# Whole 2048-column weight blocks in one cast and one subtraction, an opening over sixteen tiles, and decay rows by way of DRAM

## The chip, the cores and the metric

The kernel runs on one core of one Trainium2 chip. The metric is the device time of one execution in microseconds (us), the median of three runs. The engines are named as in the profile: PE is TensorE (PEld its weight loads), DVE is VectorE, ACT is ScalarE, SP is SyncE, which issues all DMAs here.

## What is computed

A trunk of two layers on 256 tokens of width 1024, in float32. Each layer has three sub-layers: a SwiGLU feed-forward of width 2816, a token mixer, and a second feed-forward. Each sub-layer is normalised, shifted and scaled by vectors that depend on a conditioning vector c, and added back through a gate. Cut to what matters here:

```python
def modulate(h, shift, scale):
    return h * (1 + scale[:, None, :]) + shift[:, None, :]

def swiglu(h, w13, w2):
    a, b = jnp.split(h @ w13, 2, axis=-1)
    return (jax.nn.silu(a) * b) @ w2

# layer 0: FFN half, mixer A/B (pooling + chunked state space), FFN half
# layer 1: FFN half, latent attention, FFN half
# c -> silu(c) @ mod_w[layer] + mod_b[layer]: nine vectors of 1024 per layer

# in the state-space mixer, per head and chunk of 128 tokens:
a_cs = jnp.cumsum(adt, axis=-1)
decay = jnp.exp(jnp.where(causal, a_cs[..., :, None] - a_cs[..., None, :], -jnp.inf))
```

## The kernel before

**Layout.** Activations lie transposed: channel on the partition, 256 tokens along the free axis, so a 1024-wide vector is 8 chunks. All weights are read once, in blocks of 128 x 2048 float32 (1 MB, sixteen 128 x 128 tiles), in the order of one list, `items` (lines 94 to 129). An item "w" is a weight block, "m" a block of `mod_w` (two halves of 1024 columns, one per chunk of one modulation vector), "f" a block that is used as it is. SP loads items in order into `RAHEAD` = 6 buffers `raw` (`issue_dma`, line 168).

**Splitting.** A float32 weight is used as a high part and a rest. `process_half` (line 188) takes half a "w" block: ACT casts 1024 columns into `wh` (line 217), DVE subtracts to get `wl` (line 218); each half has its own pair of buffers, 5 of each. For an "m" half, DVE multiplies it by silu(c) and sums along the row (line 204). `take` (line 239) hands out the next tile to PE and first sees that 4 pieces (halves) from the current one on have been written out in the program (`LOOK`). The order of instructions on an engine is then set by a planner with a cost model, by readiness and program order; line 207 pins each "m" product behind the vector instruction ahead of it in the program.

**Matmuls.** Most projections take three passes of 256 columns per tile (`mm3`, lines 254 to 256); the down projections two, of 512 and 256 (`mm2`, lines 260 and 261).

**The opening.** `first_pairs` (line 443) starts the first feed-forward before its modulation is complete. For each of four blocks of two chunks it waits for the four "m" halves of that block, scales and shifts two chunks (lines 397, 457), splits them (lines 308, 309) and multiplies eight output tiles by full-precision float32 products straight from an "f" block (line 465). The squares for the norm are summed by eight float32 products with a matrix of ones (line 315, called from `rms_r`). `ffn` (line 473) then goes through the 22 pairs of output tiles; the first four pairs are there already, the rest take `lin` twice. The vector c is loaded as a copy to all 128 partitions (line 148).

**The decay rows.** In `mixer_ab` (line 547), the cumulative sums of 16 heads are transposed to 16 rows (line 641), split into `ath` and `atl` (lines 643, 644), and for each head two PE products with a selecting column (lines 711, 712) spread the head's row over 128 partitions in PSUM. `heads` (line 705) makes the decay matrices from it on ACT (lines 718 to 722) and DVE (line 723), `ymm` (line 727) uses them. `heads`, tiles of z, and `ymm` take turns in the loop of line 772.

The lines of the list that set the start:

```python
    for b in range(4):
        items.append(mod_block(0, 1, b))
        items.append(mod_block(0, 0, b))
        items.append(("f" if b < NATIVE else "w", w13s[b], 4 * NS))
```

Of the kernel before, what the change touches and what calls it, by code (L numbers as in the profile page):

```python
# [17 lines left out]
P = 128  # L18
# [12 lines left out]
NS = 4  # L31
NATIVE = 4
# [6 lines left out]
MODS = (11, 10, 3, 0, 8, 8, 8, 8, 3, 1, 4)  # L39
# [22 lines left out]
def trunk(ctx, tc, xT, c_row, pos, kc, cols, rows, mod_w, w13s, w13, w2, win_a, wdt,  # L62
# [8 lines left out]
    sp = ctx.enter_context(tc.tile_pool(name="sp", bufs=4))  # L71
    pp = ctx.enter_context(tc.tile_pool(name="pp", bufs=8, space=bass.MemoryType.PSUM))
# [18 lines left out]
    def mod_block(l, v, b):  # L91
        return ("m", l, v, b)
# [68 lines left out]
    RAHEAD = 6  # L161
    PT = 8
    raws = {}
    state = {"dma": 0, "item": 0, "half": 0, "pin": False}
# [3 lines left out]
    def issue_dma(upto):  # L168
        while state["dma"] < min(upto, len(items)):
# [3 lines left out]
            if it[0] in "wf":  # L173
                nc.sync.dma_start(r[:, : it[2] * P], it[1])
            else:
                nc.sync.dma_start(r, mod_w[it[1], it[2], it[3]])
            raws[i] = r
            state["dma"] = i + 1
            if i == 15:
                late_loads()  # L180
# [7 lines left out]
    def process_half():  # L188
# [10 lines left out]
        if it[0] == "m":  # L199
            _, l, v, b = it  # L200
            c0 = l * 72 + v * 8 + b * 2 + hf
# [7 lines left out]
            if last:  # L209
                done_mod[(l, v, b)] = True  # L210
# [26 lines left out]
    LOOK = 4  # L237

    def take(m=1):
        if cur["off"] == 0:  # L240
            while len(pieces) < cur["piece"] + LOOK and process_half():
                pass
        wh, wl, n = pieces[cur["piece"]]
        o = cur["off"]
        cur["off"] += m
        assert cur["off"] <= n
        if cur["off"] == n:
            cur["piece"] += 1
            cur["off"] = 0
# [19 lines left out]
    def mod_col(l, v, part=ALL):  # L269
        lo, hi = part  # L270
        assert done_mod.get((l, v, hi // 2 - 1)), (l, v)
# [79 lines left out]
    class Norm:  # L351
# [30 lines left out]
        def sum_squares(self):  # L382
            sq = [tmp(f"sq{self.key}_{c}") for c in range(NC)]
            for c in range(NC):
                A.activation(sq[c], xt[:, c], AF.Square)  # L385
            self.r = rms_r(self.key, sq, 1.0 / D)
# [54 lines left out]
    NU = 3  # L441

    def first_pairs(norm):
        pts = [ps(f"n{m}") for m in range(2 * NS)]
        h32 = [slab(9 + q, f"h32_{q}", F32, [4, S]) for q in range(2)]
        for b in range(4):
            while not done_mod.get((0, 0, b)):
                process_half()
            if b == 0:
                norm.sum_squares()  # L450
            norm.gs = prep_scale(0, 0, (2 * b, 2 * b + 2))
            norm.sh = prep_shift(0, 0, (2 * b, 2 * b + 2))
            hs = []
            for c in (2 * b, 2 * b + 1):
                t = norm.scaled(c)
                h = h32[c // 4][:, c % 4]
                A.activation(h, t, AF.Identity, bias=norm.sh[:, c : c + 1])
                split(hh[:, c], hl[:, c], h)
                hs.append(h)
# [789 lines left out]
```

## Time and profile before

| what | us |
|---|---|
| median of 3 runs (1047.49 to 1048.79) | 1048.3 |
| the profiled execution | 1047.39 |
| its span | 1045.6 |
| PE busy | 1021.7 (98% of the span) |
| DVE busy | 837.1 (80%) |
| ACT busy | 569.0 (54%) |
| DMA | 253.46 MB, mean 242 GB/s |

The span is the time from the first to the last instruction of the profiled execution; the time of the execution is 1.8 us more. A busy PE means that some matmul is under way, and matmuls overlap, so the time that one of them takes on PE is read from the distance of starts in the timeline, not from its length.

### The profile page before, as it was taken

How to read it: one execution, taken by the hardware profiler on the slowest of the kernel's cores; microseconds unless marked ns; L12 is line 12 of the kernel's file. 1: busy time of each engine (PE TensorE's matmuls, PEld its weight loads, DVE VectorE, ACT ScalarE, POOL GpSimd, SP SyncE). 2: the span in 40 equal slices, each digit the busy share in tenths (PEclk: the TensorE clock that was granted, in tenths of full speed). 3: DMA queues.
4: the chain of work that ended last, by engine and by line, in shares of the span. 5: the costliest groups of instructions: out<-in, count | busy, mean ns of one | idle time of the engine just before them, and what ended most of it. 6: DMA issues, size and time to landing. Idle time of an engine off the chain costs nothing.

```text
span 1045.6 us, 18361 instructions
## 1 busy us (share of the span) xinstructions
PE 1021.7 (98%) x7386; PEld 955.3 (91%) x7386; DVE 837.1 (80%) x1508; ACT 569.0 (54%) x978; POOL 0.2 (0%) x4
## 2 busy tenths in 40 slices
PE   5999999999999999999999999999999999999997
PEld 4899998899888999998899999988988799999986
DVE  5788889989989897778879777899888689666553
ACT  3444454458786554445446444454678665444542
POOL 0000000000000000000000000000000000000000
PEclk9999999999999999999999999999999999999999
DMA  9999889965543577768875777798643246656501
GB/s 376 404 351 326 319 293 348 342 229 191 204 160 121 170 266 290 280 248 325 286 267 197 290 271 287 253 340 323 242 155 129 81 162 242 235 211 238 173 32 41
DMA packets 36102, 253.46 MB, mean 242 GB/s; under 512 B 4144, under 2 KB 4656, under 8 KB 5680
## 3 DMA queue, kind: packets, MB, share of 16 engines
q1 hardware_dynamic: 36016, 252.28, 65.8%
q8 instruction: 58, 0.95, 0.3%
q14 instruction: 28, 0.23, 0.1%
HBM read 251.22 MB, written 1.05 MB: 241 GB/s over the span
## 4 chain that ended last, share of the span: by engine, by line
PE 91%; DVE 5%; ACT 2%; DMA 1%; issue 0%; SPq 0%; DVEq 0%; ACTq 0%
PE f L260 16%; PE f L261 8%; PE a L254 7%; PE b L255 7%; PE b L254 7%; PE b L256 7%; PE a L256 7%; PE a L255 7%; PE o L260 3%; DVE raw L204 2%; PE o L261 2%; PE s L990 1%; DVE wl L218 1%; PE u_a L255 1%; PE u_a L254 1%; PE u_b L255 1%
## 5 line engine op out<-in xcount | busy, mean ns | idle before, releaser
L218 DVE TENSOR_TENSOR wl<-raw,wh 128x1024 fp32r<-128x1024 f32 x321 | 389.3, 1218 | 120.9 <-ACT wh L217 114.2
L217 ACT CAST wh<-raw 128x1024 fp32r<-128x1024 f32 x321 | 333.0, 1047 | 219.2 <-issue 89.0
L260 PE MATMUL f<-g,wh 128*128 128x512 f32 x704 | 248.9, 399 | 0.0
L261 PE MATMUL f<-g,wl 128*128 128x256 f32 x704 | 197.7, 281 | 0.0
L204 DVE SCALAR_TENSOR_TENSOR raw<-raw,c_bc 128x1024 f32<-128x1024 f32 x144 | 172.8, 1216 | 8.9 <-ACT sq L385 8.9
L254 PE MATMUL a<-hx,wl 128*128 128x256 f32 x600 | 170.0, 284 | 0.0
L255 PE MATMUL b<-hx,wh 128*128 128x256 f32 x600 | 169.8, 283 | 0.0
L256 PE MATMUL b<-hx,wh 128*128 128x256 f32 x600 | 169.8, 283 | 0.0
L254 PE MATMUL b<-hx,wl 128*128 128x256 f32 x600 | 169.8, 283 | 0.0
L256 PE MATMUL a<-hx,wh 128*128 128x256 f32 x600 | 169.7, 283 | 0.0
L255 PE MATMUL a<-hx,wh 128*128 128x256 f32 x600 | 169.5, 283 | 0.0
L260 PEld LDWEIGHTS f<-g,wh 128*128 128x128 f32 x704 | 132.3, 188 | 32.9
L261 PEld LDWEIGHTS f<-g,wl 128*128 128x128 f32 x704 | 133.0, 189 | 0.0
L254 PEld LDWEIGHTS a<-hx,wl 128*128 128x128 f32 x600 | 115.1, 192 | 0.6 <-ACT hx L391 0.6
L256 PEld LDWEIGHTS b<-hx,wh 128*128 128x128 f32 x600 | 115.2, 192 | 0.0
L255 PEld LDWEIGHTS b<-hx,wh 128*128 128x128 f32 x600 | 115.2, 192 | 0.0
L254 PEld LDWEIGHTS b<-hx,wl 128*128 128x128 f32 x600 | 115.2, 192 | 0.0
L256 PEld LDWEIGHTS a<-hx,wh 128*128 128x128 f32 x600 | 115.1, 192 | 0.0
L255 PEld LDWEIGHTS a<-hx,wh 128*128 128x128 f32 x600 | 115.1, 192 | 0.0
L504 ACT ACTIVATE s<-a 128x256 f32<-128x256 f32 x75 | 28.7, 383 | 94.6 <-PE a L256 94.6
L308 ACT CAST g<-g 128x256 fp32r<-128x256 f32 x88 | 35.4, 404 | 35.8 <-DVE g L505 27.1
L260 PE MATMUL o<-hx,wh 128*128 128x512 f32 x128 | 45.4, 398 | 0.0
(382 smaller groups left out, 1601.1 us busy)
## 6 DMA issues: line engine op xcount, KB each, us to landing
raw<-in_w SPq DMA_DIRECT2D x128, 1024.0 KB, 5.1
raw<-in_mod_w SPq DMA_DIRECT2D x72, 1024.0 KB, 5.3
raw<-in_win_a SPq DMA_DIRECT2D x12, 1024.0 KB, 6.6
raw<-in_wout_a SPq DMA_DIRECT2D x6, 1024.0 KB, 7.1
raw<-in_wq SPq DMA_DIRECT2D x5, 1024.0 KB, 4.9
raw<-in_w13s SPq DMA_DIRECT2D x4, 1024.0 KB, 10.3
raw<-in_win_m SPq DMA_DIRECT2D x4, 1024.0 KB, 7.1
raw<-in_wo SPq DMA_DIRECT2D x4, 1024.0 KB, 4.8
```

Source lines behind the costliest of these rows:

```text
L204: V.scalar_tensor_tensor(out=sl, in0=sl, scalar=1.0, in1=c_bc, op0=ALU.mult, op1=ALU.mult, accum_out=modc[:, c0 : c0 + 1])
L217: A.copy(wh[:, :n], src)
L218: V.tensor_tensor(out=wl[:, :n], in0=src, in1=wh[:, :n].bitcast(F32), op=ALU.subtract)
L254: T.matmul(pt, wl, xh, start=first, stop=False)
L255: T.matmul(pt, wh, xl, start=False, stop=False)
L256: T.matmul(pt, wh, xh, start=False, stop=last)
L260: T.matmul(pt, wh, x, start=first, stop=False)
L261: T.matmul(pt[:, S:], wl, x[:, 0], start=False, stop=last)
L308: A.copy(dh, src)
L504: A.activation(s, pa[:, :S], AF.Silu)
L990: T.matmul(pts[e][:, lo : lo + n], q[:, lo : lo + P], kk[:, 0:n], start=True, stop=False)
```

## The change

- A "w" block is cast by one instruction of 2048 columns and subtracted by one, into buffers of 8 KB, three of each; `LOOK` becomes 2 blocks. Inside the opening the work is still issued by halves (`fine`), into the same block buffers. `RAHEAD` becomes 5.
- `first_pairs` is rewritten: sixteen output tiles (eight pairs), issued in an order written out by hand and kept (`manual_schedule`). The first two chunks come one by one, each with its own halves of scale and shift; for eight tiles they are multiplied in full precision, for the other eight from a split block. The blocks of chunks 2 to 7 take three passes for all sixteen tiles. c is loaded as one row and spread by two PE products with ones; three and fourteen products with ones are added ahead of and behind the sum of squares; part of the squares goes to DVE.
- The decay rows: `acT` is written to DRAM and read back to all partitions, 8 heads per DMA, into `uh` and `ul`, which are free at that time; the selecting products go.
- `MODS` starts with (10, 11) in place of (11, 10): one "m" block moves from the first up projection to the first down projection.

The diff, cut to its core:

```diff
-NS = 4
-NATIVE = 4
+NS = 8
+NSETS = 2
...
+MODS = (10, 11, 3, 0, 8, 8, 8, 8, 3, 1, 4)
 NQ = 3
...
     cp = ctx.enter_context(tc.tile_pool(name="cp", bufs=1))
-    wp = ctx.enter_context(tc.tile_pool(name="wp", bufs=5))
...
+    def mod_block(l, v, b, halves=(0, 1)):
+        return ("m", tuple((l, v, b, h) for h in halves))
 
     items = []
-    for b in range(4):
-        items.append(mod_block(0, 1, b))
-        items.append(mod_block(0, 0, b))
-        items.append(("f" if b < NATIVE else "w", w13s[b], 4 * NS))
+    for c in range(2):
+        items += [("m", ((0, 1, 0, c), (0, 0, 0, c))), ("f", w13s[0, 0][:, 8 * P * c : 8 * P * c + 8 * P], 8)]
+    items.append(("w", w13s[1, 0], 16))
+    for b in range(1, 4):
+        items += [mod_block(0, 1, b), mod_block(0, 0, b)]
+        items += [("w", w13s[q, b], 16) for q in range(NSETS)]
...
     V.memset(wdtr, 0.0)
 
-    nc.sync.dma_start(c_bc, c_row.partition_broadcast(P))
+    crow = slab(10, "crow", F32, [D])[0:1]
+    nc.sync.dma_start(crow, c_row)
+    for q in range(2):
+        nc.sync.dma_start(xt[:, 4 * q : 4 * q + 4], xT[:, 4 * q : 4 * q + 4])
     nc.sync.dma_start(colt, cols)
-    A.activation(c_bc, c_bc, AF.Silu)
-    nc.sync.dma_start(xt, xT)
...
         nc.sync.dma_start(wkrr, wkr)
 
...
-            lo, hi = hf * PT, min((hf + 1) * PT, it[2])
-            n = (hi - lo) * P
-            wh = wp.tile([P, PT * P], F32R, tag="wh", name=f"wh{i}_{hf}")
-            wl = wp.tile([P, PT * P], F32R, tag="wl", name=f"wl{i}_{hf}")
-            src = r[:, lo * P : hi * P]
-            A.copy(wh[:, :n], src)
-            V.tensor_tensor(out=wl[:, :n], in0=src, in1=wh[:, :n].bitcast(F32), op=ALU.subtract)
-            pieces.append((wh, wl, hi - lo))
-            last = hi == it[2]
+            n = it[2]
+            lo, hi = (hf * PT, hf * PT + PT) if state["fine"] else (0, n)
+            if lo == 0:
+                cur["pair"] = [wp.tile([P, 2 * PT * P], F32R, tag=t, name=f"{t}{i}") for t in ("wh", "wl")]
+            wh, wl = cur["pair"]
+            o = slice(lo * P, hi * P)
+            A.copy(wh[:, o], r[:, o])
+            V.tensor_tensor(out=wl[:, o], in0=r[:, o], in1=wh[:, o].bitcast(F32), op=ALU.subtract)
+            pieces.append((wh, wl, lo, hi))
+            last = hi == n
...
-    LOOK = 4
+    LOOK = 2
+    state["look"] = LOOK
...
+    W0, W1 = 3, 14
 
     def first_pairs(norm):
-        pts = [ps(f"n{m}") for m in range(2 * NS)]
-        h32 = [slab(9 + q, f"h32_{q}", F32, [4, S]) for q in range(2)]
-        for b in range(4):
-            while not done_mod.get((0, 0, b)):
+        state["look"] = 1
+        wm = ps("warm")
+
+        def warm(n):
+            for _ in range(n):
+                T.matmul(wm[:, :P], onesf, onesf, start=True, stop=True)
+
+        def silu_c(q):
+            pt = ps(f"c{q}")
...
+            o = slice(512 * q, 512 * q + 512)
+            T.matmul(pt, onesf[0:1, :], crow[:, o], start=True, stop=True)
+            A.activation(c_bc[:, o], pt, AF.Silu)
+
+        warm(W0)
+        sq = [tmp(f"sq{c}") for c in range(NC)]
+        silu_c(0)
+        for c in (0, 1):
+            A.activation(sq[c], xt[:, c], AF.Square)
+        silu_c(1)
+        for c in (4, 5):
+            A.activation(sq[c], xt[:, c], AF.Square)
+        warm_sqrt("first")
...
+        for i, c in enumerate((0, 1, 2, 4, 5, 6)):
+            T.matmul(pss[:, :S], onesf, sq[c], start=i == 0, stop=i == 5)
+        warm(W1)
+        process_half()
+        r = sp.tile([P, S], F32, tag="r", name="r_first", bufs=2)
+        q = sp.tile([P, S], F32, tag="rq", name="rq_first", bufs=1)
+        v = sp.tile([P, 8], F32, tag="rv", name="rv_first", bufs=2)
+        V.transpose(q, pss[:, :S])
+        A.activation(v, q.rearrange("p (b j) -> p b j", j=32)[:, :, 0], AF.Sqrt, bias=eps_t[:, 0:1], scale=1.0 / D)
+        process_half()
+        V.reciprocal(v, v)
+        V.transpose(r.rearrange("p (b j) -> p b j", j=32), v.unsqueeze(2).to_broadcast([P, 8, 32]))
...
+        def scaled(c):
+            m, b = mod_col(0, 1, (c, c + 1))
+            g = gs_t[:, 0, c : c + 1]
+            V.scalar_tensor_tensor(out=g, in0=m, scalar=b1[:, c : c + 1], in1=colt[:, CP_NG + c : CP_NG + c + 1],
+                                   op0=ALU.add, op1=ALU.mult)
+            t = tmp(f"h{norm.key}_{c}")
+            V.tensor_tensor(out=t, in0=xt[:, c], in1=r, op=ALU.mult)
+            sh = prep_shift(0, 0, (c, c + 1))[:, c : c + 1]
+            A.activation(h[c], t, AF.Identity, bias=sh, scale=g)
+            A.copy(hh[:, c], h[c])
...
+        def low(c):
+            V.tensor_tensor(out=hl[:, c], in0=h[c], in1=hh[:, c].bitcast(F32), op=ALU.subtract)
...
+        def part(q, b):
+            for m in range(8 * q, 8 * q + 8):
+                for k in (2 * b, 2 * b + 1):
+                    wh, wl = take()
+                    for w, x in ((wl, hh), (wh, hl), (wh, hh)):
+                        T.matmul(tile_of(m), w, x[:, k], start=k == 0 and m % 2 == 0 and w is wl,
+                                 stop=k == NC - 1 and w is wh and x is hh, skip_group_check=True)
...
+        for c in range(2):
+            if c:
                 process_half()
+                process_half()
+            scaled(c)
+            w = next_raw()
+            for m in range(8):
+                T.matmul(tile_of(m), w[:, m * P : (m + 1) * P], h[c], start=c == 0 and m % 2 == 0, stop=False,
+                         skip_group_check=True)
+            release_raw()
+        low(0)
+        low(1)
+        process_half()
+        process_half()
+        part(1, 0)
+        for b in range(1, 4):
+            process_half()
+            process_half()
+            process_half()
+            scaled(2 * b)
+            process_half()
+            low(2 * b)
+            scaled(2 * b + 1)
+            process_half()
+            low(2 * b + 1)
+            for q in range(NSETS):
+                part(q, b)
+        while len(pieces) < cur["piece"] + 2:
+            process_half()
+        state["look"], state["fine"] = LOOK, False
+        norm.gs, norm.sh = gs_t[:, 0], sh_t[:, 0]
+        return [tile_of(m) for m in range(2 * NS)]
...
-        ath, atl = wd[0:16, 1], wd[0:16, 2]
-        V.tensor_copy(ath, pT[0:16, :S])
-        V.tensor_tensor(out=atl, in0=pT[0:16, :S], in1=ath.bitcast(F32), op=ALU.subtract)
+        acT = sp.tile([16, S], F32, tag="acT", name="acT", bufs=1)
+        V.tensor_copy(acT, pT[0:16, :S])
+        acd = dp.tile([1, 16, S], F32, name="acd")
+        nc.sync.dma_start(acd[0], acT)
+        rows_ = [t[:, :, :S].bitcast(F32) for t in (uh, ul)]
+        for q in range(2):
+            nc.sync.dma_start(rows_[q], acd[0:1, 8 * q : 8 * q + 8].partition_broadcast(P))
...
-                row = ps(f"row{h}")
-                sel = identr[0:16, h : h + 1].to_broadcast([16, P])
-                T.matmul(row[:, :S], sel, atl, start=True, stop=False)
-                T.matmul(row[:, :S], sel, ath, start=False, stop=True)
+                row = rows_[h // 8][:, h % 8]
...
-    pts = first_pairs(n)
+    with tc.manual_schedule(engines={mybir.EngineType.PE, mybir.EngineType.DVE, mybir.EngineType.Activation}):
+        pts = first_pairs(n)
```

## Rows read from the trace of the kernel before

**Rows 1.** The page of the profile: busy time and chain.

```profile
PE 1021.7 (98%) x7386; PEld 955.3 (91%) x7386; DVE 837.1 (80%) x1508; ACT 569.0 (54%) x978; POOL 0.2 (0%) x4
...
PE 91%; DVE 5%; ACT 2%; DMA 1%; issue 0%; SPq 0%; DVEq 0%; ACTq 0%
```

**Rows 2.** Waits of PE: who was waited for, us in total, times, longest.

```profile
PE ss L315 <- ACT sq L385: 8.3, 1, 8.3
PE n L465 <- ACT h L457: 5.8, 3, 4.5
...
PE o L1018 <- ACT pT L1012: 0.6, 2, 0.3
```

**Rows 3.** Timeline of the opening: start, length, engine, line, operation, count.

```profile
7.82 2.56 ACT L385 ACTIVATE sq<-xt 128x256 f32<-128x256 f32 x8 [1.87 <-DMA xt<-in_xT]
...
8.29 5.41 PE L315 MATMUL ss<-sq,onesf 128*128 128x256 f32 x16 [8.29 <-ACT sq L385]
...
18.16 15.77 PE L465 MATMUL n<-h,raw 128*128 128x256 f32 x64 [4.46 <-ACT h L457]
```

**Rows 4.** Timeline of PE: a native stretch, and starts of looped pairs.

```profile
42.49 7.17 PE L465 MATMUL n<-h,raw 128*128 128x256 f32 x32 [0.94 <-ACT h L457]
...
55.25 0.28 PE L254 MATMUL a<-hx,wl 128*128 128x256 f32 x1
...
72.53 0.28 PE L254 MATMUL a<-hx,wl 128*128 128x256 f32 x1
```

**Rows 5.** Windows: stretch, busy (count) of each engine, granted clock, DMA share, GB/s.

```profile
2.00:7.80 5.80, 0.00 (x0) 0.00 (x0) 0.00 (x0) 1.06 (x2) 0.00 (x0) 1.00 1.01 347
8.00:18.00 10.00, 5.41 (x16) 4.19 (x16) 6.89 (x16) 4.37 (x11) 0.00 (x0) 1.00 1.01 427
19.00:22.00 3.00, 3.00 (x9) 2.37 (x8) 2.96 (x7) 0.11 (x1) 0.00 (x0) 0.50 1.03 426
22.00:26.00 4.00, 4.00 (x21) 3.51 (x19) 3.57 (x9) 0.29 (x1) 0.00 (x0) 1.00 1.02 422
```

**Rows 6.** Timeline of DVE: subtractions of 256 and of 1024 columns.

```profile
35.05 0.76 DVE L309 TENSOR_TENSOR hx<-h,hx 128x256 fp32r<-128x256 f32 x2 [1.27 <-ACT hx L308]
...
48.88 2.35 DVE L218 TENSOR_TENSOR wl<-raw,wh 128x1024 fp32r<-128x1024 f32 x2
```

**Rows 7.** Timeline of PE in the first mixer: rows of two heads.

```profile
286.85 0.38 PE L711 MATMUL row<-wd,identr 16*128 16x256 f32 x1
...
287.52 0.38 PE L254 MATMUL z<-hx,wl 128*128 128x256 f32 x1
```

**Rows 8.** Windows: first down projection and mixers, columns as in Rows 5.

```profile
153.00:216.00 63.00, 63.00 (x361) 54.71 (x361) 58.97 (x94) 28.23 (x39) 0.00 (x0) 1.00 0.90 336
...
285.00:310.00 25.00, 24.89 (x184) 20.32 (x183) 20.25 (x47) 19.57 (x57) 0.00 (x0) 1.00 0.46 169
310.00:335.00 25.00, 24.08 (x139) 19.83 (x138) 23.13 (x59) 18.34 (x38) 0.00 (x0) 1.00 0.29 98
750.00:778.00 28.00, 26.28 (x190) 24.53 (x189) 25.00 (x60) 22.80 (x52) 0.00 (x0) 1.00 0.53 189
778.00:822.00 44.00, 43.38 (x334) 36.97 (x334) 38.53 (x119) 35.85 (x101) 0.00 (x0) 1.00 0.34 121
```

**Rows 9.** Timelines around the decay rows; DMA landings 240 to 320.

```profile
249.09 0.41 DVE L643 CAST wd<-acsT 16x256 fp32r<-16x256 f32 x1
...
254.11 9.19 SPq L174 DMA_DIRECT2D raw<-in_win_a  x2
...
273.77 0.38 PE L711 MATMUL row<-wd,identr 16*128 16x256 f32 x1
...
raw<-in_wout_a SPq DMA_DIRECT2D x6, 1024.0 KB, 7.1
```

**Rows 10.** Timeline of ACT: casts of weight halves early in the feed-forward.

```profile
45.66 1.04 ACT L217 CAST wh<-raw 128x1024 fp32r<-128x1024 f32 x1
...
64.37 1.99 ACT L217 CAST wh<-raw 128x1024 fp32r<-128x1024 f32 x2
```

More of the change, by code (lines that the diff above doesn't have):

```diff
@@ L38 @@
 SKIP0 = 3
-MODS = (11, 10, 3, 0, 8, 8, 8, 8, 3, 1, 4)
+MODS = (10, 11, 3, 0, 8, 8, 8, 8, 3, 1, 4)
 NQ = 3
@@ L159, in late_loads @@
         nc.sync.dma_start(wkrr, wkr)
-    RAHEAD = 6
+    RAHEAD = 5
     PT = 8
     raws = {}
-    state = {"dma": 0, "item": 0, "half": 0, "pin": False}
+    state = {"dma": 0, "item": 0, "half": 0, "pin": False, "fine": True}
     pieces, parked, held = [], [], []
@@ L175, in issue_dma @@
             else:
-                nc.sync.dma_start(r, mod_w[it[1], it[2], it[3]])
+                (l, v, b, h0), other = it[1]
+                if other == (l, v, b, h0 + 1):
+                    nc.sync.dma_start(r, mod_w[l, v, b])
+                else:
+                    for e, (l, v, b, h) in enumerate(it[1]):
+                        nc.sync.dma_start(r[:, e * D : e * D + D], mod_w[l, v, b][:, h * D : h * D + D])
             raws[i] = r
             state["dma"] = i + 1
-            if i == 15:
+            if i == 20:
                 late_loads()
@@ L236, in trunk @@
     cur = {"piece": 0, "off": 0}
-    LOOK = 4
+    LOOK = 2
+    state["look"] = LOOK
     def take(m=1):
         if cur["off"] == 0:
-            while len(pieces) < cur["piece"] + LOOK and process_half():
+            while len(pieces) < cur["piece"] + state["look"] and process_half():
                 pass
-        wh, wl, n = pieces[cur["piece"]]
-        o = cur["off"]
+        wh, wl, lo, hi = pieces[cur["piece"]]
+        o = lo + cur["off"]
         cur["off"] += m
-        assert cur["off"] <= n
-        if cur["off"] == n:
+        assert lo + cur["off"] <= hi
+        if lo + cur["off"] == hi:
             cur["piece"] += 1
@@ L270, in mod_col @@
         lo, hi = part
-        assert done_mod.get((l, v, hi // 2 - 1)), (l, v)
+        assert all(done_mod.get((l, v, c)) for c in range(lo, hi)), (l, v)
         o = l * 72 + v * 8
@@ L382, in sum_squares @@
         def sum_squares(self):
-            sq = [tmp(f"sq{self.key}_{c}") for c in range(NC)]
+            ss = sp.tile([P, S], F32, tag="ss", name=f"ss{self.key}", bufs=2)
             for c in range(NC):
-                A.activation(sq[c], xt[:, c], AF.Square)
-            self.r = rms_r(self.key, sq, 1.0 / D)
+                sq = tmp(f"sq{self.key}_{c}") if c else ss
+                A.activation(sq, xt[:, c], AF.Square)
+                if c:
+                    V.tensor_tensor(out=ss, in0=ss, in1=sq, op=ALU.add)
+            return ss
         def h(self, c):
@@ L441, in trunk @@
     NU = 3
+    W0, W1 = 3, 14
     def first_pairs(norm):
-        pts = [ps(f"n{m}") for m in range(2 * NS)]
-        h32 = [slab(9 + q, f"h32_{q}", F32, [4, S]) for q in range(2)]
-        for b in range(4):
-            while not done_mod.get((0, 0, b)):
-                process_half()
[L449 to L459, printed above, removed]
-            if b < NATIVE:
-                w = next_raw()
-                for m in range(2 * NS):
-                    for k in range(2):
-                        o = (2 * m + k) * P
-                        T.matmul(pts[m][:, :S], w[:, o : o + P], hs[k], start=b + k == 0, stop=b + k == 4)
-                release_raw()
-                continue
-            for m in range(2 * NS):
-                for k in (2 * b, 2 * b + 1):
-                    mm3(pts[m][:, :S], take(), hh[:, k], hl[:, k], False, k == NC - 1)
@@ new lines, in first_pairs @@
+        for c in (0, 1):
[4 more added lines that the diff above has]
+        warm_sqrt("first")
+        for c in (2, 6):
+            for k in (c, c + 1):
+                V.tensor_tensor(out=sq[k], in0=xt[:, k], in1=xt[:, k], op=ALU.mult)
+            V.tensor_tensor(out=sq[c], in0=sq[c], in1=sq[c + 1], op=ALU.add)
+        b1 = sp.tile([P, 8], F32, tag="b1", name="b1", bufs=1)
+        V.tensor_scalar(out=b1, in0=colt[:, CP_MODB + 8 : CP_MODB + 16], scalar1=1.0, scalar2=None, op0=ALU.add)
@@ new lines, in first_pairs @@
+        process_half()
+        V.reciprocal(v, v)
+        V.transpose(r.rearrange("p (b j) -> p b j", j=32), v.unsqueeze(2).to_broadcast([P, 8, 32]))
+        norm.r = r
+        pts = [ps(f"n{j}") for j in range(NS)]
+        h32 = slab(9, "h32", F32, [4, S])
+        h = [h32[:, c % 4] for c in range(NC)]
+        def scaled(c):
[8 more added lines that the diff above has]
+            A.copy(hh[:, c], h[c])
@@ L557, in mixer_ab @@
         sz = [sz_[:, i] for i in range(4)] + [bc[:, i] for i in range(4)]
-        identr = sp.tile([P, P], F32R, tag="identr", name="identr", bufs=1)
-        V.tensor_copy(identr, ident)
         wdh, wdl = wd[:, 0, :240], wd[:, 3, :240]
```

21 lines of the change are left out of this document (13 added, 8 removed).

## The prediction

> **What bounds the kernel now.** I read the busy shares and the chain first: PE is busy for 98% of the span, and the chain that ended last runs over PE for 91% of it [rows 1]. So time is gained in two ways only: PE is made to wait less, or given less to do. The waits of PE come next [rows 2]: 8.3 us before the first sum of squares and 5.8 us in three waits for the first scaled chunks are nearly all of it; the rest of the trace has single waits of a microsecond or less. PE's idle time is thus in the first 50 us and in the output at the end, which the change leaves alone. The timeline of the opening [rows 3] says why it starts late: x lands and is squared from 7.82, eight products with ones run on PE to 13.7, then DVE and ACT transpose, modulate and scale, and the first real product starts at 18.16, after a wait of 4.46 for ACT. The granted clock was 0.50 from 19 to 22, that is, 1.2 GHz, after PE had stood idle from 13.7 to 18.16; it was 1.00 from 22 on [rows 5].
>
> **Durations.** Distances of starts count. A full-precision product of 256 columns is two records; 32 records in 7.17 us give 0.448 us for one [rows 4]. A pair of output tiles by three passes costs (72.53 - 55.25) / 3 = 5.76 us, 48 passes of 0.12; one tile 0.36 [rows 4]. On DVE, 1024 columns cost 2.35 - 1.22 = 1.13 us from start to start and 256 columns 0.76 - 0.42 = 0.34 (the length of one record being 0.42) [rows 6]; the line through both is 0.075 us plus 1.03 ns per column, so 2048 columns are about 2.19 us. ACT casts 1024 columns in 0.95 from start to start [rows 10] and does 256 in 0.32 [rows 3].
>
> **The opening, start.** DMA moved 347 GB/s from 2.0 to 7.8 and 427 after [rows 5]. By 7.8, when x was there, 2.05 MB had been moved, while x and what stood ahead of it are 1.72; I take a transfer as landed 0.33 MB after its own last byte. The new order is c's row, two halves of x, the columns, then 0.52 MB pieces. That gives x at 4.9 and 6.3, the first scale piece at 7.9, shift 9.2, weights 10.4, the second chunk's pieces 11.7, 12.9 and 14.1, the first split block 16.6, and 2.5 us for each MB after it. Of the squares ACT does four and DVE four; the last is ready at about 7.7. Eight products with ones took 5.41 us [rows 3], 0.68 each; six, with only the last waiting, end between 8.7 and 10.3; I take 9.1, since most are done while x's second half is on its way. DVE then runs transpose 0.45, the shift product 1.13, reciprocal and second transpose 0.6, scaling 0.6, with ACT's root and scaling, 0.3 and 0.45, between: the first real product starts at about 12.6 (11.8 to 14.5). The fourteen products with ones are half as wide as those of rows 4: 14 x 0.224 = 3.1 us, from 9.1 to 12.2. They lie in the wait and cost nothing; at half clock they would end at 15.4 and then be the later of the two. The spread of c by PE (two products of 512 columns, 0.9 us each, twice that at half clock) starts at about 2.8 and ends by 6.4, before the first scale piece lands.
>
> **The opening, PE's work.** For the first two chunks 16 full-precision products, 7.2 us; the other eight tiles of those chunks, 16 x 0.36 = 5.8; three rounds of 32 tile steps, 3 x 11.5 = 34.6. Sum 47.5. Before, the same eight pairs took 64 x 0.448 = 28.7 plus four looped pairs, 23.0, sum 51.7, with waits and slow clock from 18.16 to 72.53 [rows 4]. Will DVE keep up? A round has four modulation halves and four weight halves, 8 x 1.13, two scalings of about 0.6 and two rests of 0.34: 10.9 us against PE's 11.5. DMA needs 4 x 2.5 = 10 us a round. Both fit, narrowly. The first round starts late: the split block lands at 16.6, its second half is subtracted by 19.9, then four modulation halves, two scalings, one rest and one weight half come to 27.3, while PE has run out at 12.6 + 7.2 + 5.8 = 25.6. PE waits about 1.8 us. After that DVE is ahead. Eight pairs are finished at 27.3 + 34.6 = 62, against 72.5: 10.5 us less. For semaphore hand-offs, which the chain has in number, I take off 0.5: **-10.0 us**; bounds -13.5 (start at 11.8, no wait) and -5.5 (start at 14.5, 4 us of waits).
>
> **The decay rows.** Four row products sit between the transposes and z: from 286.85 to 287.52, 0.67 us for two heads, eight times, 5.4 us [rows 7]. About 0.08 of it is the change of kind of matmul and stays: 4.7 us. PE is the bound of that stage with DVE at 20.25 of 25.0 us and ACT at 19.57 [rows 8]. A step shrinks from 4.9 to 4.3 us, so DVE is at 93%; from 310 on, DVE is at 23.1 of 25 and the last two heads have no z tile behind them, so their share (1.2 us) may be lost. I take **-4.3**, bounds -5.4 and -1.3. The DMAs: the sums are ready at about 249.5, the first row is used at 273.8 [rows 9]. SP must wait for them and for the write to land; 1 MB took 7.1 us in this stretch [rows 9], so one write and two reads are over by 249.5 + 3 x 7.1 = 271 at most. Weight loads stand behind SP meanwhile; SP already stood 9.19 us in one place there [rows 9] and PE had no wait for it. The Trainium skill, in DMA: Bandwidth & Descriptors (Two DMAs through the same engine are not ordered; Anatomy of one DMA), speaks against this detour: a DMA that reads what another wrote must wait for its semaphore, and each pays about 2.0 us fixed; by that estimate the rows come at about 258 and not 271, and rival (3) below would be half as likely as I hold it. No row of before shows a write followed by a read.
>
> **Whole blocks.** 161 pairs of halves become one each, less the few in the opening: DVE saves 0.075 us for each, about 11 us in all, ACT about as much. Neither is the bound, so this earns nothing where PE is full. What it can cost is delay: a short operation can stand 2.2 us instead of 1.13 behind a subtraction. Cover is the lead of the casts. The ninth and tenth casts start at 64.37 with eight from 45.66 ahead of them [rows 10]; PE needs them at 72.53 [rows 4], 6.2 us after the second cast ends. The casts run as far ahead as their five buffers let them. Three blocks hold six halves, so this lead stays. PE has little cover in the second mixer, where it was busy 26.28 of 28 and 43.38 of 44 us with DVE at 25.0 and 38.5 [rows 8]. There the cost is between -1.7 (its waits vanish) and +4 (four more exposed delays of 1.07); I take **+0.5**. The modulation block moved into the down projection adds 2.3 us to DVE, 58.97 of 63 busy [rows 8], less 11 x 0.075; it fits, and costs 2.3 at most if it did not. Five raw buffers instead of six: the 22 loads of that stage took 63 us [rows 8], 2.9 each, so five are 14 us of cover for a landing of 7.1 [rows 9] and a subtraction; that costs nothing.
>
> **Sum.** -10.0 - 4.3 + 0.5 = -13.8. The profiled execution took 1047.4 (span 1045.6 and 1.8 around it), giving 1033.6. The median of the three is 0.9 more: **1034.5 us**, own range 1029 to 1040.
>
> **Rivals.** (1) *DVE becomes the bound.* In the mixer with rows removed, and in the rounds of the opening, which leave 0.6 us each; the heads' gain is lost and the opening gives its lower bound: 1048.3 - 5.5 - 1.3 = 1041.5. For: DVE's shares above. Against: PE's chain. (2) *Slower: long instructions in front of short ones.* Eight steps of heads, eight of attention and forty residual chunks each have a short operation for which PE waits soon after. If the extra 1.07 us is exposed at half of these 56, it costs 30 us: 1064. It decides from 13 of them on, where it eats the 14 us. Against it: before, subtractions of 1.13 us lie in all these places and PE waited 0.6 us in two places for one attention copy [rows 2], so delays are mostly covered. (3) *The rows come late.* If SP issues the write only behind two such waits of 9.19 us, reading ends near 290 and PE stands some 8 us: 1042.5. Against: the margin above. (4) *Better:* both lower bounds and no waits in the second mixer: 1027.5.
>
> **Chances.** Forecast 0.70, (1) 0.14, (2) 0.06, (3) 0.04, (4) 0.06. The range 1028 to 1043 takes in the forecast, (1) and (3) and leaves out (2) and most of (4). About 0.2% (2 us) is what a measurement of this kernel can tell from no change: faster by more 0.90, within 0.04, slower 0.06.
>
> **What would show it.** The first product on the modulated chunks starts near 12.6 and the ninth pair near 62; granted clock 1.00 throughout; no line 711 or 712, and steps of heads of 4.3 us; PE's waits between 62 and the end below 4 us in sum. I am wrong if PE starts after 15, if a wait of PE for a split block appears in the feed-forwards, or if the reads of the rows land after the first head needs them.

## The result, and the profile after

The changed kernel takes **1059.9 us** in the median (1057.9 to 1061.7), the kernel before 1048.55 in the same runs: ratio 1.0109, 95% interval 1.0087 to 1.0132. 1034.5 with 1028 to 1043 was forecast. The profiled execution took 1061.7, the longest of its four; its span is 1059.9 (1045.6 before). So the spans, from which the stages below are read, differ by 14.3, the medians by 11.4.

The page of the kernel after (busy time, chain, two groups) and its waits of PE answer to [rows 1] and [rows 2]. Line numbers are those of each kernel's own text; the cast of a weight block is L225 here, its subtraction L226.

```profile
PE 1028.2 (97%) x7436; PEld 961.7 (91%) x7436; DVE 833.6 (79%) x1368; ACT 556.3 (52%) x827; POOL 0.2 (0%) x4
...
PE 80%; DVE 11%; ACT 5%; DMA 2%; issue 1%; SPq 0%; DVEq 0%; ACTq 0%
...
L226 DVE TENSOR_TENSOR wl<-raw,wh 128x2048 fp32r<-128x2048 f32 (+1 forms) x172 | 374.7, 2182 | 112.6 <-ACT wh L225 112.2
L225 ACT CAST wh<-raw 128x2048 fp32r<-128x2048 f32 (+1 forms) x172 | 312.5, 1823 | 286.5 <-PE b L265 130.2
```

```profile
PE n L525 <- DVE wl L226: 5.8, 3, 4.4
PE o L269 <- DVE hx L318: 5.5, 1, 5.5
PE o L1105 <- ACT pT L1099: 5.1, 2, 3.5
PE s L1077 <- DVE qh L1068: 2.6, 1, 2.6
...
PE f L270 <- DVE wl L226: 0.7, 1, 0.7
```

DVE and ACT are less busy than before, as the change intends; yet PE's share of the chain fell from 91 to 80%, and DVE's rose from 5 to 11. The first wait is in the opening. The next three, 13.2 us, are new or grown: at the first mixer's tail (`o`, the output projection, on `hx`, the split of the gated chunks) and in the second mixer (on `pT`, the transposed attention weights, and `qh`, the rotated queries). The last is in the first down projection. The granted clock fell behind the three. The windows of the kernel after (columns as in [rows 5]):

```profile
316.00:320.00 4.00, 0.75 (x2) 0.65 (x3) 4.00 (x7) 1.69 (x6) 0.00 (x0) 0.63 0.21 27
320.00:324.00 4.00, 4.00 (x14) 3.34 (x13) 3.49 (x12) 1.30 (x4) 0.00 (x0) 0.51 0.58 236
772.00:776.00 4.00, 1.43 (x10) 1.19 (x9) 3.88 (x7) 2.53 (x3) 0.00 (x0) 0.81 0.99 293
776.00:780.00 4.00, 4.00 (x16) 3.21 (x16) 3.29 (x9) 0.69 (x1) 0.00 (x0) 0.50 0.83 315
780.00:784.00 4.00, 4.00 (x31) 4.00 (x30) 2.93 (x6) 3.06 (x10) 0.00 (x0) 0.84 0.72 242
828.00:832.00 4.00, 4.00 (x20) 2.91 (x20) 1.77 (x7) 1.04 (x4) 0.00 (x0) 0.63 0.73 262
```

From 776 to 780 PE is busy all the time at 1.2 GHz and gets through 16 records; from 780, partly at 2.4 GHz, 31. Summing one minus the clock over windows of 4 us gives the full-speed work lost: 3.4 us in the first mixer and 5.1 in the second. Before, no window of either was below 1.00.

Stages by the start of their first product on PE (tile views), one execution each, with the median of each run, say where the 14.3 us arose. The mixers run from `u_B` to the next `u_a`, and from `u_kv` to the last `u_a`. All but the first two are experiments, described below.

| kernel | first down projection starts | first mixer | second mixer | median |
|---|---|---|---|---|
| before | 153.2 | 132.0 | 120.6 | 1048.55 |
| after | 151.0 | 136.2 | 131.0 | 1059.9 |
| e2_whole | 154.8 | 135.6 | 131.8 | 1065.1 |
| e3_rows | 153.5 | 129.2 | 120.5 | 1044.4 |
| e4_open | 150.7 | 132.9 | 120.5 | 1045.9 |
| e1_halves | 151.0 | 128.6 | 123.7 | 1045.95 |
| e12_five | 150.2 | 128.7 | 120.5 | 1041.0 |
| e5_halves46 | 150.6 | 129.9 | 120.8 | 1041.65 |
| e6_pairs | 150.5 | 127.2 | 123.3 | 1045.5 |
| e10_subhalves | 151.0 | 127.7 | 122.5 | 1045.5 |
| e11_casthalves | 150.8 | 130.9 | 122.2 | 1052.1 |
| e14_mla | 150.8 | 136.3 | 122.4 | 1052.3 |
| e7_mixhalves | 151.0 | 131.7 | 123.8 | 1048.6 |
| e13_fill_tail | 150.6 | 134.0 | 131.9 | 1058.2 |
| e8_early | 149.6 | 128.4 | 120.5 | 1041.1 |
| e9_fill | 147.7 | 130.4 | 120.5 | 1038.65 |

After against before: -2.2 up to the first down projection, +0.8 in it, +4.2 in the first mixer (the decay rows' gain already in it), -0.2 between the mixers, +10.4 in the second, +1.3 behind it: 14.3. Between the mixers the feed-forwards are as they were; the 0.8 of the first down projection is its wait for a split block, 0.7 us.

### The profile page after: what moved, and what is told of

The parts are those of the page before. It is cut to its first block, busy times and chain, and to the rows that moved or that the text cites. A ratio compares the mean times of both kernels' runs of the same rounds, so it can differ in the third digit from the quotient of the medians.

```text
span 1059.9 us, 18127 instructions
## 1 busy us (share of the span) xinstructions
PE 1028.2 (97%) x7436; PEld 961.7 (91%) x7436; DVE 833.6 (79%) x1368; ACT 556.3 (52%) x827; POOL 0.2 (0%) x4
## 4 chain that ended last, share of the span: by engine, by line
PE 80%; DVE 11%; ACT 5%; DMA 2%; issue 1%; SPq 0%; DVEq 0%; ACTq 0%
PE f L269 12%; PE a L263 6%; PE b L265 6%; PE b L264 6%; PE b L263 6%; PE a L265 6%; PE a L264 6%; PE f L270 6%; DVE wl L226 4%; PE o L269 3%; DVE raw L212 3%; ACT wh L225 2%; PE o L270 2%; DMA raw<-in_w13s 1%; PE n L525 1%
## 5 line engine op out<-in xcount | busy, mean ns | idle before, releaser
L226 DVE TENSOR_TENSOR wl<-raw,wh 128x2048 fp32r<-128x2048 f32 (+1 forms) x172 | 374.7, 2182 | 112.6 <-ACT wh L225 112.2
L225 ACT CAST wh<-raw 128x2048 fp32r<-128x2048 f32 (+1 forms) x172 | 312.5, 1823 | 286.5 <-PE b L265 130.2
L269 PEld LDWEIGHTS f<-g,wh 128*128 128x128 f32 x704 | 132.1, 188 | 32.5
L265 PE MATMUL b<-hx,wh 128*128 128x256 f32 x568 | 160.7, 283 | 0.0
L264 PE MATMUL b<-hx,wh 128*128 128x256 f32 x568 | 160.7, 283 | 0.0
L263 PE MATMUL a<-hx,wl 128*128 128x256 f32 x568 | 160.6, 283 | 0.0
L263 PE MATMUL b<-hx,wl 128*128 128x256 f32 x568 | 160.6, 283 | 0.0
L265 PE MATMUL a<-hx,wh 128*128 128x256 f32 x568 | 160.6, 283 | 0.0
L264 PE MATMUL a<-hx,wh 128*128 128x256 f32 x568 | 160.6, 283 | 0.0
L264 PEld LDWEIGHTS b<-hx,wh 128*128 128x128 f32 x568 | 109.1, 192 | 0.0
L265 PEld LDWEIGHTS b<-hx,wh 128*128 128x128 f32 x568 | 109.1, 192 | 0.0
L263 PEld LDWEIGHTS b<-hx,wl 128*128 128x128 f32 x568 | 109.0, 192 | 0.0
L265 PEld LDWEIGHTS a<-hx,wh 128*128 128x128 f32 x568 | 109.0, 192 | 0.0
L264 PEld LDWEIGHTS a<-hx,wh 128*128 128x128 f32 x568 | 109.0, 192 | 0.0
L593 DVE TENSOR_TENSOR g<-b,s 128x256 f32<-128x256 f32 x71 | 29.9, 422 | 39.3 <-PE b L265 39.3
```

What stands on the lines that cost most here:

```text
L225: A.copy(wh[:, o], r[:, o])
L226: V.tensor_tensor(out=wl[:, o], in0=r[:, o], in1=wh[:, o].bitcast(F32), op=ALU.subtract)
L263: T.matmul(pt, wl, xh, start=first, stop=False)
L264: T.matmul(pt, wh, xl, start=False, stop=False)
L265: T.matmul(pt, wh, xh, start=False, stop=last)
L269: T.matmul(pt, wh, x, start=first, stop=False)
```

## Experiments

The expectations name five theories. Theory 1: long instructions stand in front of short ones in the mixers. 2: five load buffers instead of six starve PE. 3: the decay rows' way through DRAM holds up what follows. 4: the opening is held by its order on ACT and DVE. 5: it is held by loads that come late.

**The three parts, each alone on the kernel before.** e2_whole is these lines; e3_rows takes the diff's lines on `acd` and `rows_`; e4_open its `items`, `MODS`, `first_pairs` and squares, with halves in the old buffers.

```
-    wp = ctx.enter_context(tc.tile_pool(name="wp", bufs=5))
+    wp = ctx.enter_context(tc.tile_pool(name="wp", bufs=3))
...
-    RAHEAD = 6
-    PT = 8
+    RAHEAD = 5
+    PT = 16
...
-    LOOK = 4
+    LOOK = 2
```

> The kernel before with whole 2048-column casts and subtractions alone (three 8 KB buffers, look-ahead of two blocks, five buffers for loads); its opening and its decay rows by TensorE are kept. Theory 1: it pays the mixers' loss without the gains of the other parts, 1060 to 1068 us. Theory 3 (the loss belongs to the decay rows or the opening): 1047 to 1050 us. Theory 2 (load buffers) expects the same as theory 1 here and is told from it by the kernel with halves in these buffers.

> The kernel before with the decay rows by way of DRAM alone. By the prediction's term -4.3 us (bounds -5.4 to -1.3): 1044.2 us, 1043 to 1047. Theory 3 (the way through DRAM holds up the heads or the tail of the first mixer): 1049 to 1055 us. If the gain is given back at the mixer's tail, whose products wait for the second group's norm whatever the heads do: 1048 to 1049 us.

> The kernel before with the new opening alone: halves in five 4 KB buffers, six buffers for loads, decay rows by TensorE. The changed kernel's trace has the eight pairs done 2.0 us earlier than before, where 10 was forecast. Theory 4 (the opening is held by its order on ScalarE and VectorE, each round 13.1 us, whatever the buffers): 1046 to 1047.5 us, ninth pair at about 70.5 us. Theory 5 (it is held by loads that come late with five buffers): the sixth buffer gives back 3 to 6 us, 1041 to 1044 us, ninth pair at 64 to 67 us.

Ratios: e2_whole 1.0163 (1.0148 to 1.0179), e3_rows 0.9962 (0.9947 to 0.9977), e4_open 0.9979 (0.9970 to 0.9989). In microseconds +17.0, -3.7 and -2.2, in sum +11.1; the whole change gave +11.4. In the total the parts add up, and the whole blocks are the loss. By stage they add up less well: the first mixer's changes sum to +1.7 (+3.6, -2.8, +0.9), and the whole change gave +4.2. The wait of 5.5 us on `hx` isn't in e2_whole at all and came only in kernels with all three parts, so the close agreement of the totals is in part luck. Theory 3 falls: in e3_rows the z tiles of the first mixer end at 300.4 instead of 305.1. For the opening theory 4 stands, and theory 5 falls as far as it is about buffers: a sixth changes nothing (ninth pair at 70.1).

**Halves again, in three forms of buffer.** e1_halves is the changed kernel with `LOOK = 4` halves and `fine` left on, in its 8 KB buffers; e5_halves46 has the old five 4 KB buffers and six load buffers; e12_five has `RAHEAD = 5` in e5_halves46.

```
-    LOOK = 2
+    LOOK = 4
...
-        state["look"], state["fine"] = LOOK, False
+        state["look"] = LOOK
```

> The changed kernel with one thing undone: every weight block is cast and subtracted in two 1024-column halves again (four halves of look-ahead), in the same three 8 KB buffers and with the same five buffers for loads. Theory 1 (long instructions stand in front of short ones in the two mixers: the trace after lost about 7 us between 300 and 350 us and 12 us between 756 and 868 us): those 19 us come back less about 1 us for 86 more of each instruction's fixed cost, so 1041 to 1046 us. Theory 2 (five buffers for loads, not six, starve PE): nothing comes back, 1058 to 1061 us. Theory 3 (the decay rows' way through DRAM holds up what follows): the part before 350 us stays lost, 1047 to 1053 us.

> The new opening and the decay rows by DRAM, with the weight blocks as before (two 1024-column halves in five 4 KB buffers, six buffers for loads). If the parts add up (-2.2 us for the opening alone and -3.7 us for the rows alone): 1042.2 us. The kernel with halves in three 8 KB buffers and five buffers for loads gave 1046.0 and lost 3.1 us in the second mixer's 120 us, which neither part alone shows: if the buffers are its cause, those 3.1 us are back here (second mixer 120.5 us); if the two parts together are, 1045 to 1046.

> The kernel with opening and decay rows and halves as before (1041.7 us), with five buffers for loads instead of six; halves stay in five 4 KB buffers. The kernel with halves in three 8 KB buffers and five load buffers took 1046.0. If the missing load buffer is the cause of these 4.3 us: 1045 to 1046.5, the second mixer at 123.5 us. If the form of the 8 KB buffers is (a half is freed only with its partner): 1041.5 to 1042.5, the second mixer at 120.5.

e1_halves is at 0.9979 (0.9969 to 0.9990): 14 us come back with the same five load buffers, so theory 2 falls. e5_halves46 is at 0.9940 (0.9926 to 0.9953), e12_five at 0.9932 (0.9915 to 0.9948). So five load buffers cost nothing, as I had predicted, while halves in 8 KB pairs cost 4 to 5 us against halves in buffers of their own, 3.2 of them in the second mixer. That an 8 KB buffer comes free only when both halves are used is my explanation; no run tests it.

**Length or grain, and whose.** Grain is how much is handed over at a time. e6_pairs hands blocks over whole but casts and subtracts each in two halves; e10_subhalves halves the subtraction alone (the lines below), e11_casthalves the cast alone.

```
+            for a in range(lo, hi, PT):
+                o = slice(a * P, min(a + PT, hi) * P)
                 V.tensor_tensor(out=wl[:, o], in0=r[:, o], in1=wh[:, o].bitcast(F32), op=ALU.subtract)
```

> The changed kernel, each block still handed over whole (same look-ahead of two blocks, same three 8 KB buffers, same five buffers for loads), but by two 1024-column casts and two 1024-column subtractions that follow one another. Theory 1a (the length of one instruction does the harm: a short instruction waits for at most one half): 1046 to 1049 us. Theory 1b (the grain does it: 4 us of work of VectorE come up at a time, and short work stands behind all of it, in one instruction or two): 1057 to 1062 us. Second mixer by 1a 124 to 126 us, by 1b 131 us (changed kernel 131.0).

> The changed kernel with the whole-block cast kept (1.82 us) and the subtraction alone in two halves. Where both were halved (block still handed over whole) it took 1045.5, with both whole 1059.9. If VectorE's long instruction does the harm: 1046 to 1049. If ScalarE's does (its cast stood ahead of a square and of the activations of the tail): 1056 to 1060. If each carries a part: 1050 to 1055.

> The changed kernel with the cast alone in two halves and the whole-block subtraction kept (2.18 us). The mirror of the run with the subtraction in halves: VectorE's length 1056 to 1060, ScalarE's 1046 to 1049, both 1050 to 1055.

e6_pairs 0.9982 (0.9973 to 0.9991), e10_subhalves 0.9979 (0.9970 to 0.9988), e11_casthalves 1.0038 (1.0023 to 1.0053). The same work in the same buffers, but in instructions of 1.22 us instead of 2.18, takes 14.4 us less (13 by the ratios): the length of one instruction does it, not the grain. The subtraction's length is enough: with it halved the long cast costs nothing. But halving the cast alone brings back 7.8 too: 8.8 in the second mixer and 5.3 in the first, less 2.9 lost in the first down projection, where PE now waits for split blocks. So the two lengths work together. The chain of the kernel after in the second mixer, start and length; first ahead of PE's wait on `qh`, from 772.6 to 775.2, then ahead of its wait on `pT`, from 824 to 827.5:

```profile
769.40 2.19 DVE wl L226
...
772.39 2.21 DVE wl L226
...
774.63 0.43 DVE qh L1068
```

```profile
812.84 0.26 ACT qr L1058
813.11 1.82 ACT wh L225
814.95 2.29 DVE wl L226
817.24 0.33 DVE rtq L1007
817.58 0.33 DVE qr L1008
...
818.27 0.42 DVE qh L1068
```

In the first piece two long subtractions stand among the short operations that lead to `qh`. In the second, DVE's next short operation, `rtq`, needs the rotation product, which ran on PE from 814.39 to 814.98. DVE had been idle for 1.32 us; the long cast ended just before that product did, so the long subtraction slipped in and `rtq` stood behind it until 817.2. With the subtraction halved, in the chain of e14_mla at the same place, 1.23 us follow the cast and not 2.29:

```profile
809.42 1.82 ACT wh L225
811.27 1.23 DVE wl L229
812.49 0.33 DVE rtq L1011
```

At the first mixer's tail, the timeline of DVE in the kernel after (start, length, and in brackets the idle time before and who ended it), and then that of e1_halves:

```profile
303.46 0.44 DVE L340 STREAM_TRANSPOSE rq_g<-ss_g 128x256 f32<-128x256 f32 x1
...
308.62 0.16 DVE L350 TENSOR_TENSOR nw_g<-nw_g 128x8 f32<-128x8 f32 x1
308.69 2.29 DVE L226 TENSOR_TENSOR wl<-raw,wh 128x2048 fp32r<-128x2048 f32 x1
310.89 0.16 DVE L351 TENSOR_TENSOR nw_g<-nw_g 128x8 f32<-128x8 f32 x1
...
315.90 0.42 DVE L835 TENSOR_TENSOR gss<-gss,gsq 128x256 f32<-128x256 f32 x1 [1.13 <-ACT gsq L834]
316.24 2.28 DVE L226 TENSOR_TENSOR wl<-raw,wh 128x2048 fp32r<-128x2048 f32 x1
318.44 0.42 DVE L835 TENSOR_TENSOR gss<-gss,gsq 128x256 f32<-128x256 f32 x1
318.78 0.42 DVE L318 TENSOR_TENSOR hx<-xs,hx 128x256 fp32r<-128x256 f32 x1
```

```profile
300.72 0.45 DVE L340 STREAM_TRANSPOSE rq_g<-ss_g 128x256 f32<-128x256 f32 x1
...
312.17 1.22 DVE L226 TENSOR_TENSOR wl<-raw,wh 128x1024 fp32r<-128x1024 f32 x1
313.30 1.43 DVE L318 TENSOR_TENSOR hx<-xs,hx 128x256 fp32r<-128x256 f32 x4
```

A chain of some twenty short operations on DVE and ACT leads to `hx`. Two long subtractions land in it, and ahead of the second ACT's cast (313.65 to 315.5) held up the squares; the chain that ended last runs over this cast and the second subtraction. From `rq_g` to `hx` it takes 15.3 us after, 12.6 in e1_halves. PE waits 5.5 for `hx` after, and 0.7 in e1_halves, with 1.6 for the sum of squares just ahead.

**Where.** e14_mla halves the subtraction for the second mixer's weights alone (these carry a fourth element, below); e7_mixhalves hands over halves in the two mixers and whole blocks in the feed-forwards.

```
+            step = PT if len(it) > 3 else 2 * PT
+            for a in range(lo, hi, step):
+                o = slice(a * P, min(a + step, hi) * P)
```

> The changed kernel with the subtraction in two halves for the second mixer's weights alone (whole casts everywhere, whole subtractions elsewhere). With halved subtractions everywhere the second mixer took 122.5 us instead of 131.0 and the whole 1045.5 instead of 1059.9. If each mixer pays for its own blocks: the second mixer 122 to 124 us, the first stays at 136, in all 1051 to 1053. If the harm in the second mixer came with what is queued from outside (modulation halves, the next feed-forward's blocks): the second mixer 127 to 131, in all 1056 to 1060.

> The changed kernel with halves in the two mixers alone; the feed-forwards keep whole blocks. Theory 1 (only the mixers, where PE has little cover, pay for whole blocks): 1045 to 1047 us, first mixer about 128.6 us, second 124 us, feed-forwards unchanged. If the feed-forwards' turns into the mixers carry a part of the harm (whole blocks queued at the seams): 1048 to 1055 us.

e14_mla: 1.0039 (1.0024 to 1.0053), second mixer 122.4, first unchanged at 136.3: each mixer pays for its own blocks. e7_mixhalves, at 1048.6 and 1.0003 (0.9994 to 1.0012), missed theory 1 by 2 us and lies in the range given for whole blocks queued at the turns into the mixers. Its first mixer is 3.1 us longer than in e1_halves, its second as long. 1.7 us of full-speed work were lost to a fall of the clock behind the first mixer's tail (0.57 from 316 to 320). The other 1.5 us arise ahead of the last z tile; whether whole blocks at the turn are their cause is open.

**How much is the clock.** e13_fill_tail puts 22 products of ones with a zero tile into the wait at the first mixer's tail.

```
+        for _ in range(22):
+            T.matmul(proj.pts[OPEN_A - 1][:, :P], onesf, zerof, start=False, stop=False, skip_group_check=True)
         proj.cut(1)
```

> The changed kernel with 22 products of ones with a zero tile (0.235 us each, 5.2 us) put behind the sum of squares at the first mixer's tail, where PE waited 5.5 us for the split of the gated chunks and the granted clock then was 0.63 and 0.51 in the next 8 us (3.4 us of full-speed work). They change no sum. If the clock's fall is a cost of its own beside the wait: the clock stays at 1.00 there and 2.5 to 3.5 us come back, 1056 to 1057.5, first mixer 133 us instead of 136.2. If the tail is held by VectorE and ScalarE whatever the clock: 1059 to 1061.

Its windows:

```profile
316.00:320.00 4.00, 3.39 (x25) 2.96 (x24) 3.99 (x9) 0.77 (x4) 0.00 (x0) 1.00 0.32 84
320.00:324.00 4.00, 4.00 (x24) 3.49 (x23) 3.87 (x12) 1.88 (x5) 0.00 (x0) 1.00 0.42 178
```

The clock stays at 1.00 (0.63 and 0.51 after), and PE gets through 24 records from 320 to 324 instead of 14. The first mixer falls by 2.2 us, to 134.0. The whole time, 1058.2 and 1.0099 (1.0084 to 1.0114), lies between the two ranges expected, and its gain of 1.7 us within the intervals; the second mixer of this execution lost 6.8 us of full-speed work, where it lost 5.1 in the kernel after. So the clock's fall is a cost of its own, in this stage 2 of the 7 us that lie between the kernel after and e3_rows (129.2).

**The opening.** e8_early is e5_halves46 with the first weight half of each round cast ahead of its activation tiles; e9_fill adds 18 products with a zero tile behind the first split part.

```
         for b in range(1, 4):
+            A.copy(cur["tiles"][0], raws[i][:, : PT * P])
```

> The kernel with opening and decay rows but halves as before, and one more edit in the opening: in each of its three rounds ScalarE casts the first weight half before it makes the round's two activation tiles, not behind them. In the traces with the new opening each round takes 13.07 us on VectorE, of which it idles 2.05 us for that cast. Theory 4 (this hand-over sets the round): the round falls to PE's 11.5 us, the ninth pair starts near 65 us instead of 70, and the whole takes 4 to 6 us less than the kernel without the edit (1036 to 1039 us). Theory 5 (the loads set the round): the idle time moves to the loads, under 1 us is gained.

> The kernel with the early cast in the opening's rounds, and 18 products of ones with a zero tile (128 columns, 0.235 us each by the trace of the changed kernel, 4.2 us in all) added to a PSUM tile behind the first split part: they fill the wait of 4.7 us there and change no sum. In the trace without them the granted clock is 0.55 from 30 to 35 us and 0.77 from 35 to 40, behind that wait, which is some 3.4 us of full-speed work. If the fall of the clock is what took the early cast's gain: the clock stays at 1.00, the ninth pair starts at 65.5 to 66.5 instead of 69.0, and the whole takes 2.5 to 3.5 us less, 1037.5 to 1038.6 us. If the rounds are held by something else (DVE's 11.6 us, the loads): the ninth pair at 68 to 69 and 1040.5 to 1041.5.

Timelines of DVE in e4_open and in e8_early, the first subtractions of two rounds:

```profile
31.04 1.23 DVE L224 TENSOR_TENSOR wl<-raw,wh 128x1024 fp32r<-128x1024 f32 x1 [2.05 <-ACT wh L223]
...
44.11 1.22 DVE L224 TENSOR_TENSOR wl<-raw,wh 128x1024 fp32r<-128x1024 f32 x1 [2.06 <-ACT wh L223]
```

```profile
30.65 1.22 DVE L226 TENSOR_TENSOR wl<-raw,wh 128x1024 fp32r<-128x1024 f32 x1
...
42.24 1.22 DVE L226 TENSOR_TENSOR wl<-raw,wh 128x1024 fp32r<-128x1024 f32 x1
```

Of the idle time 0.5 us a round are left, and the round falls from 13.07 to 11.6 us, as theory 4 says. Yet the ninth pair comes at 69.0 instead of 69.9, and 0.9933 (0.9921 to 0.9946) isn't told apart from e5_halves46, where 4 to 6 us had been expected. PE was behind by then. Windows of e8_early, and of e9_fill:

```profile
30.00:35.00 5.00, 2.99 (x14) 3.02 (x15) 4.48 (x8) 3.85 (x5) 0.00 (x0) 0.55 1.01 419
35.00:40.00 5.00, 5.00 (x35) 5.00 (x35) 5.00 (x10) 1.05 (x1) 0.00 (x0) 0.77 1.01 416
```

```profile
30.00:35.00 5.00, 4.20 (x36) 4.04 (x35) 4.42 (x8) 3.88 (x6) 0.00 (x0) 1.00 1.01 421
35.00:40.00 5.00, 5.00 (x44) 5.00 (x43) 5.00 (x9) 1.05 (x1) 0.00 (x0) 1.00 1.02 415
```

With the wait filled the clock stays at 1.00, the ninth pair starts at 67.1 (0.6 us later than expected), and the time is **1038.65 us**, 0.9915 (0.9900 to 0.9929) of before. It has the lowest median here, though its interval overlaps those of e8_early and e12_five: opening and decay rows kept, whole blocks undone, two edits in the opening. The wait itself stays: ACT's early cast stood until 28.0 for the transfer of that weight block, with the DMA engines at 415 to 421 GB/s.

## Why the prediction was wrong

**Whole blocks: the step that failed.** I took +0.5, with +4 as the upper bound; the part cost 17.0 alone. With all three parts in, whole blocks cost 18.9 (1059.9 against 1041.0 in e12_five): 14.4 go with the subtraction's length, and the rest is about what halves in 8 KB buffers cost. I bounded the mixers by four more delays of 1.07 us, each by itself. The traces show long instructions that stand in one chain of short operations (a cast and two subtractions in the first mixer's tail; two subtractions, and a cast with a subtraction behind it, in the second mixer), so that delays add up before PE meets them: waits of 5.5, 3.5 and 2.6 us and not of one. I also looked for cover in the lead of the casts [rows 10], which says when weights are ready. In the mixers that did no harm: PE's long waits there are for `hx`, `pT` and `qh`. In the first down projection, for which I had added nothing (2.3 us at most), a sign of being wrong that I had named did come: a wait of 0.7 us for a split block. The question was what else stands in DVE's and ACT's queues.

**Rival (2)** was the right mechanism, at a chance of 0.06 that was far too low. Its size was of another make: not 1.07 us at half of 56 places, but a few long waits and the clock behind them; for the residual chunks only two short ones, 0.5 and 0.2 us, behind the second mixer. My argument against it was that subtractions of 1.13 us cost only 0.6 us in these places [rows 2]. It said nothing of 2.2 us, and it left out a row of the same view:

```profile
PE s L990 <- DVE qh L981: 1.0, 1, 1.0
```

Three subtractions of 1.13 us already stood in the chain to `qh` before (764.99, 766.68 and 767.89), and PE waited for it. In the kernel after, this wait is the one of 2.6.

**The clock** was left out of every wait. [rows 5] showed 0.50 after an idle stretch of 4.46 us, and I still priced a wait at its own length. The Trainium skill, in TensorE: Matmul & The Clock Gate (Part 1: The HAM clock gate), says that an idle PE is let down to 1.2 GHz. The runs agree where the clock was 0.50 from 776 to 780, behind a wait of 2.6 us, and filling two of the waits kept 1.00; but not every wait had a fall behind it (last section).

**The opening** gained 2.2 instead of 10. By my terms: first product at 14.33 instead of 12.6 (+1.7), 13.7 us to the end of the first split part instead of 13.0 (+0.7), a wait of 4.4 instead of 1.8 (+2.6), three rounds in 37.9 instead of 34.6 (+3.3); 8.3 in all, and the ninth pair at 70.4 instead of 62. The +1.7 is the sum of squares, which ended at 10.9 and not at 9.1. The end of the wait came at 32.5 instead of 27.3, and two terms make up these 5.2 us. One is the loads (+3.2): the first split block came at 19.7 and not at 16.6, so its second half was subtracted by 23.1 and not by 19.9. A window, and ACT's timeline, of the kernel after:

```profile
8.00:18.00 10.00, 9.71 (x54) 8.37 (x53) 7.23 (x18) 3.19 (x7) 0.00 (x0) 1.00 1.01 363
19.70 1.99 ACT L225 CAST wh<-raw 128x1024 fp32r<-128x1024 f32 x2 [1.42 <-DMA raw<-in_w13s]
```

I had taken 427 GB/s from the same window of the kernel before [rows 5]; here 363 were moved, at the same DMA share of 1.01. Why is open; e4_open, with six load buffers, shows 372. The other is the hand-over (+2.05): DVE's round was 11.0 of work, as I had summed, but 2.05 of idle time for the cast came on top. I had summed one engine and not the hand-overs in a fixed order. Of the last term, three rounds, the early cast took off 0.9 (36.95 in e8_early), and the filled wait, with the clock at 1.00, another 2.2 (34.8 in e9_fill, 32.3 to 67.1).

**The decay rows** were right in size, -3.7 against -4.3. In the first mixer of e3_rows 5.0 us were gained up to the last z tile, where I had 4.7 for the products that go; behind it 2.2 were lost, 1.7 us of full-speed work by a fall of the clock that I had no term for (0.96 and 0.61 from 312 to 320). That the total came out so near is in part luck. The rows' DMAs in the kernel after (length in ns, start, then us from issue to landing):

```profile
L731 SPq DMA_DIRECT2D acd<-acT x1: 333/333/333, 253.5 to 253.5; - x1
L734 SPq DMA_DIRECT2D uh<-acd x1: 383/383/383, 258.3 to 258.3; - x1
L734 SPq DMA_DIRECT2D ul<-acd x1: 574/574/574, 258.7 to 258.7; - x1
...
DMA to landing us min/median/max: 4.7/4.8/7.3
```

The write had landed by 258.3, the reads by 263.1 and 266.0. ACT's first operation on the rows had been put ahead and stood 1.5 us for the first read:

```profile
263.13 0.40 ACT L805 ACTIVATE lm<-uh,acs 128x128 f32<-128x128 f32 x1 [1.53 <-DMA uh<-acd]
```

So this sign of being wrong came too, in a small form: no wait of PE goes back to it; PE's first product with a decay matrix starts at 280.5. Rival (3) did not come. My bound of 271 was 5 us late. I had worked out 258 from the Trainium skill's fixed cost (DMA: Bandwidth & Descriptors, Anatomy of one DMA), which that section gives for DMAs that GpSimd issues; here SP issues them. It was 8 us early: 4.0 because the write was issued at 253.5 and not at 249.5, the rest because the write took 4.7 us and the second read 7.3. In e3_rows the write took 1.4 us and the reads 7.9 and 10.4.

**Feed-forwards and load buffers** were right but for the 0.7 us above: 379.0 us between the mixers against 379.2, and e12_five is no slower than e5_halves46.

## What to carry to other kernels

Merging instructions on an engine that isn't the bound saves nothing where PE is full, and lengthens every queue in which short operations stand between PE's products: price it by the longest chain of short operations that crosses the engine, not by busy shares. Price each wait of PE with the clock that falls behind it; harmless products in a wait that can't be removed kept the clock here. Try the parts of a change one by one: two of these three were gains.

## What the hardware showed

The clock's fall is not the same in each execution. At the first mixer's tail e5_halves46, e8_early, e9_fill and e12_five have the same waits of 0.7 to 0.9 us and the same 3.7 us of idle time in the stage; in the first and third the clock fell there (1.7 us of full-speed work lost), in the others it did not. Nor does the length of a wait alone decide: in the second mixer PE's wait on `qh` was 2.6 us in the kernel after, with a fall to 0.50, and 2.8 us in e11_casthalves, where every window of 4 us kept 1.00. Over whole executions time and clock go together: the four of the changed kernel took 1057.9, 1058.8, 1061.0 and 1061.7 us at a mean granted clock of 0.993, 0.992, 0.989 and 0.988. So single microseconds between two profiles can be this alone.
